# A transformer block on one core: other ends for the two sweeps of its down-projection

## Chip, cores and metric

One core of one Trainium2 chip runs the whole kernel. The metric is device time in microseconds (us); the kernel before takes 747.35 us, the median of three runs (747.33 to 748.2).

## The reference

The layer normalises x, projects it, runs two attention branches, and adds the gated result to x. Then comes the feed-forward part, with a causal convolution of width 3 over its hidden columns:

```python
def conv_glu(x, w_up, conv_w, conv_b, w_down):
    hid = x @ w_up
    hid = lax.conv_general_dilated(...) + conv_b
    gate, up = hid[..., :D_FF], hid[..., D_FF:]
    return (jax.nn.silu(gate) * up) @ w_down
...
x = x + mixed @ w_out
x = x + conv_glu(rms_norm(x, norm2_g), w_ffn_up, ffn_conv_w, ffn_conv_b, w_ffn_down)
```

x is 512 x 1024, D_FF is 2816, all float32. The case is about the last product, 512 x 2816 by 2816 x 1024, and the sum with x behind it.

## The kernel before, in words

**The product.** The 2816 rows of w_down are eleven pairs (i = 0 to 10) of 128 rows, the 1024 output columns two sweeps (s = 0, 1) of 512. One step, chunk `dn{s}_{i}`, adds the product of a 2 x 2 block matrix on either side by Strassen's scheme in Winograd's form: seven products P1 to P7 of sums of blocks instead of eight. The seven sums of the activations (`a{i}`, high and low parts) are made once, while the up-projection still runs, and serve both sweeps. Those of the weights are made per chunk.

**Precision.** Each float32 operand is split into a high part (a cast to fp32r) and a low part (the rest). A product is three matmuls: high by high (L855), high by low (L856), low by high (L857), each 128 x 128 by 128 x 256. With two halves t of the rows a product is six matmuls, a chunk 42, the stage 924. A product keeps its PSUM bank for a whole sweep, so seven of the eight banks are in use; sweep 1 takes the eighth and then those that sweep 0 has left.

**A weight chunk on its way.** SP issues its load (L100, 512 KB into `raw_dn`, two buffers). DVE forms the sums of blocks (L111 of 512 columns, L112 and L113 of 256). ACT casts the high part in two pieces, 768 and 1024 columns (L131), and DVE subtracts for the low part (L133). The 768 piece has P1, P3 and P2 and needs only the load; the 1024 piece has P5, P7, P6 and P4 and needs the sums. High and low have two buffers each (`whi`, `wlo`), so chunk c+2 can't be cast before PE is done with c. The load of chunk c+2 is issued behind the last low part of c, which frees its `raw` buffer.

**The ends of a sweep.** x (after the attention) lies in HBM as `x2d`. Four loads of 256 KB (L870) bring 512 of its columns into `xo`. When the last chunk of a sweep is done, `fin` adds the banks up into `xo`: ACT copies P1 to `u` (L891), DVE makes eleven or so adds (L884), and SP stores the result by quarters (L878, L915). `xo` has one buffer, so sweep 1's x waits for sweep 0's stores.

**The order.** The code gives only a rough order. A scheduler with a simulated timeline sets the order of each engine's instructions when the program is built; on the chip each engine keeps it strictly, and SP's loads and stores are one queue in that order. PE runs ahead with high-by-high matmuls of the next chunk where they are ready sooner than the low part. `behind(ins, others)` makes the scheduler put `ins` after `others`.

Of the kernel before, what the change touches and what calls it, by code (L numbers as in the profile page):

```python
# [8 lines left out]
F32 = mybir.dt.float32  # L9
F32R = mybir.dt.float32r  # L10
AF = mybir.ActivationFunctionType
ALU = mybir.AluOpType
# [3 lines left out]
P = 128  # L16
S = 512
D = 1024
NT = S // P
# [3 lines left out]
NP = NF // 2  # L23
# [41 lines left out]
def block_kernel(ctx: ExitStack, tc: tile.TileContext, x, xt, params, g2, rbx, wts, wdn, out):  # L65
# [25 lines left out]

    order = [key for key, _, _ in CHUNKS]

    raws, splits = {}, {}
    FIRST_DN = order.index("dn0_0")

    def load(i, parts=1):
# [10 lines left out]
    def down_sums(raw):  # L108

        b = raw.rearrange("p (b c) -> p b c", c=256)  # L110
        V.tensor_tensor(b[:, 4:6], b[:, 0:4:2], b[:, 0:2][:, ::-1], op=ALU.subtract)  # L111
        V.tensor_tensor(b[:, 6], b[:, 2], b[:, 4], op=ALU.subtract)  # L112
        V.tensor_tensor(b[:, 7], b[:, 6], b[:, 3], op=ALU.subtract)  # L113

    def split_gen(i, pieces):

        if i >= len(order):
            return
        key = order[i]
        kn = CHUNKS[i][1]  # L120
        raw = raws.pop(i)
        hi = wp.tile([P, 2048], F32R, tag="whi", name=f"whi_{key}")
        lo = wp.tile([P, 2048], F32R, tag="wlo", name=f"wlo_{key}")
        splits[key] = (hi.rearrange("p (k c) -> p k c", k=kn), lo.rearrange("p (k c) -> p k c", k=kn))
        cuts = [2048 // pieces * j for j in range(pieces + 1)]
        if i >= FIRST_DN:
            down_sums(raw)
            pieces, cuts = 2, [256, 1024, 2048]
        for j in range(pieces):
            sl = slice(cuts[j], cuts[j + 1])  # L130
            A.copy(hi[:, sl], raw[:, sl])  # L131
            E = G if i == 2 else V
            E.tensor_tensor(lo[:, sl], raw[:, sl], hi[:, sl].bitcast(F32), op=ALU.subtract)  # L133
            if j == pieces - 1 and i + 2 < len(order):
                next(load(i + 2))
            yield

    pos = {k: i for i, k in enumerate(order)}

    def run_chunk(key, body, pieces=4):  # L140

        sp = split_gen(pos[key] + 1, pieces)
        hi, lo = splits.pop(key)
        for _ in body(hi, lo):
            next(sp, None)
            yield
        for _ in sp:
            pass
# [29 lines left out]
    def ptile(tag, bufs, name):  # L178
        return pp.tile([P, S], F32, tag=tag, name=name, bufs=bufs)
# [553 lines left out]
    for _ in sp:  # L733
        pass
    ap_ctx.close()
    fp = ctx.enter_context(tc.tile_pool(name="fp", bufs=1))

# [88 lines left out]

    PRODS = (1, 6, 5, 7, 2, 4, 3)
    BLK = {1: 1, 3: 2, 2: 3, 5: 4, 7: 5, 6: 6, 4: 7}
# [4 lines left out]
    def pbank(name):  # L837
        tag = SLOTS[nslot[0] % 8]
        nslot[0] += 1
        return ptile(tag, BUFS[tag], name)  # L840

    def down_body(s, i, P_, fin):
        def body(hi, lo):
            a = pairs[i]
            for p in PRODS:
                if i == 0:
                    P_[p] = pbank(f"P{p}_{s}")
                ps = P_[p]
                for t in range(2):
                    o = 256 * OP[p] + P * t  # L850
                    sh, sl = a[:, o:o + P], a[:, 1792 + o:1792 + o + P]
                    mh, ml = hi[:, BLK[p], :], lo[:, BLK[p], :]
                    dst = ps[:, 256 * t:256 * (t + 1)]
                    first, last = i == 0, i == NP - 1
                    PE.matmul(dst, sh, mh, start=first and t == 0, stop=False, skip_group_check=True)  # L855
                    PE.matmul(dst, sh, ml, start=False, stop=False, skip_group_check=True)  # L856
                    PE.matmul(dst, sl, mh, start=False, stop=last, skip_group_check=True)  # L857
                if i == NP - 1:
                    fin(p)
                yield  # L860
        return body

    def sweep(s):
        P_ = {}
        col = 512 * s
        xt2 = fp.tile([P, NT, S], F32, tag="ub", name=f"xo{s}")

        def fetch():
            for t in range(NT):
                SP.dma_start(xt2[:, t, :], x2d[t, :, col:col + 512])  # L870

        def X(r, c):
            return xt2[:, 2 * r:2 * r + 2, 256 * c:256 * (c + 1)]

        def put(r, c):
            for t in range(2 * r, 2 * r + 2):
                cs = slice(256 * c, 256 * (c + 1))
                SP.dma_start(out[0, t * P:(t + 1) * P, col + 256 * c:col + 256 * (c + 1)], xt2[:, t, cs])  # L878

        tmp = {}  # L880
        v3 = lambda ap: ap.rearrange("p (t c) -> p t c", t=2)

        def add(o, a, b, op=ALU.add):
            V.tensor_tensor(o, a, b, op=op)  # L884

        def fin(p):
            ps = P_[p]
            p3 = v3(ps)
            if p == 1:
                tmp["u"] = fp.tile([P, S], F32, tag="cg", name=f"u2_{s}", bufs=1)  # L890
                A.copy(tmp["u"], ps)  # L891
                add(X(0, 0), p3, X(0, 0))
            elif p == 6:
                add(tmp["u"], ps, tmp["u"])
            elif p == 5:
                tmp["v"] = fp.tile([P, 768], F32, tag="st", name=f"u5_{s}", bufs=1)[:, 0:S]
                add(tmp["v"], ps, tmp["u"])
                add(X(0, 1), v3(tmp["v"]), X(0, 1))
                add(X(1, 1), v3(tmp["v"]), X(1, 1))
            elif p == 7:  # L900
                add(tmp["u"], ps, tmp["u"])
                add(X(1, 0), v3(tmp["u"]), X(1, 0))
                add(X(1, 1), p3, X(1, 1))
                put(1, 1)
            elif p == 2:
                add(X(0, 0), p3, X(0, 0))
                put(0, 0)
            elif p == 4:
                add(X(1, 0), X(1, 0), p3, op=ALU.subtract)
                put(1, 0)  # L910
            else:
                for t in range(2):
                    o = xt2[:, t, 256:512]
                    add(o, ps[:, 256 * t:256 * (t + 1)], o)
                    SP.dma_start(out[0, t * P:(t + 1) * P, col + 256:col + 512], o)  # L915

        for i in range(NP):
            if i == 6:
                fetch()
            for _ in run_chunk(f"dn{s}_{i}", down_body(s, i, P_, fin)):  # L920
                pass

    for s in range(2):
        sweep(s)


def _layout(inputs):
# [38 lines left out]
```

## Time and profile before

| what | value |
|---|---|
| median of three runs | 747.35 us |
| the profiled execution: its own time | 750.49 us |
| its span, first to last instruction | 747.8 us |
| PE busy in the span | 733.1 us (98%) |
| DVE busy | 536.0 us (72%) |
| ACT busy | 376.8 us (50%) |
| down-projection: first to last matmul start | 626.26 to 740.50 us |
| last add of DVE starts | 743.79 us |

Times on the timeline are us from the start of the span. A row of the timeline has the start, the length, the engine, the line and operation with what it writes and reads, and how many instructions stand in the row; in brackets is the idle time before it and what ended that. A line of the groups has the count, then the busy time and the mean ns of one, then the idle time before and what ended it. PE is matmul, PEld its weight load; SPq rows are the issue of a DMA, not the transfer. Busy times of matmuls overlap, so the step from one start to the next says more than their length.

### The profile page before, as it was taken

To read this page: it belongs to the slowest core of one execution; us is meant where nothing else is said; L and a number is where in the kernel's file an instruction comes from. 1 tells how busy PE (TensorE), PEld (TensorE's weight loads), DVE (VectorE), ACT (ScalarE), POOL (GpSimd) and SP (SyncE) were. 2 spreads that over 40 slices of the span, in tenths; PEclk is the share of its full clock that TensorE was granted. 3 is DMA by queue.
4 is the path that set the end of the run, shared out by engine and by line. 5 is a ranking of instruction groups with operands and counts; after the bars stand their busy time and mean duration, and the time that the engine had idled before them with its cause. 6 is when DMAs were issued, how large, how long until landed. Compare 5 with 4: busy or idle time off the path is not lost.

```text
span 747.8 us, 10959 instructions
## 1 busy us (share of the span) xinstructions
PE 733.1 (98%) x4301; PEld 645.1 (86%) x4301; DVE 536.0 (72%) x985; ACT 376.8 (50%) x671; POOL 41.8 (6%) x73
## 2 busy tenths in 40 slices
PE   9999999999999999999999999999999999998996
PEld 8999998888988888888899888888888889998896
DVE  6588876776978886573475777676668767878676
ACT  6675565557856775432254544534444433542341
POOL 2701200001011011000000000000000000000000
PEclk9999999999999999999999999999999999999999
DMA  8632232122221121235241232232133111443431
GB/s 295 250 122 85 79 116 74 61 88 79 65 106 57 57 99 71 85 113 224 114 169 61 110 112 75 96 112 103 67 113 113 61 53 57 141 142 122 159 109 62
DMA packets 19779, 79.96 MB, mean 107 GB/s; under 512 B 2192, under 2 KB 5392, under 8 KB 13584
## 3 DMA queue, kind: packets, MB, share of 16 engines
q1 hardware_dynamic: 19584, 79.18, 30.0%
q8 instruction: 33, 0.54, 0.3%
q14 instruction: 18, 0.15, 0.1%
q10 hardware_dynamic: 144, 0.10, 0.0%
HBM read 75.07 MB, written 4.19 MB: 106 GB/s over the span
## 4 chain that ended last, share of the span: by engine, by line
PE 89%; DMA 5%; DVE 4%; ACT 0%; SPq 0%; issue 0%; POOL 0%; ACTq 0%; DVEq 0%
PE pg L153 5%; PE pu L153 5%; PE pu L152 5%; PE pg L152 5%; PE pu L154 5%; PE pg L154 5%; PE P L856 3%; DMA raw_dn<-in_wdn 3%; PE P L857 3%; PE P L855 3%; PE gA L152 2%; PE wo L154 2%; PE wo L152 2%; PE wo L153 2%; PE gA L154 2%; PE qkB L152 2%
## 5 line engine op out<-in xcount | busy, mean ns | idle before, releaser
L133 DVE TENSOR_TENSOR wlo_up<-raw_up,whi_up 128x1024 fp32r<-128x1024 f32 (+1 forms) x50 | 52.4, 1093 | 49.6 <-ACT whi_up L131 49.6
L856 PE MATMUL P<-wlo_dn,a 128*128 128x256 f32 x308 | 83.2, 282 | 3.0 <-DVE wlo_dn L133 3.0
L857 PE MATMUL P<-whi_dn,a 128*128 128x256 f32 x308 | 82.8, 281 | 0.0
L855 PE MATMUL P<-whi_dn,a 128*128 128x256 f32 x308 | 76.6, 281 | 1.2 <-ACT whi_dn L131 1.2
L131 ACT CAST whi_dn<-raw_dn 128x768 fp32r<-128x768 f32 (+1 forms) x44 | 40.3, 943 | 63.2 <-PE P L857 38.2
L153 PE MATMUL pu<-htl,whi_up 128*128 128x512 f32 (+1 forms) x192 | 72.1, 375 | 0.0
L153 PE MATMUL pg<-htl,whi_up 128*128 128x512 f32 (+1 forms) x192 | 72.0, 375 | 0.0
L152 PE MATMUL pu<-hth,whi_up 128*128 128x512 f32 (+1 forms) x192 | 71.7, 374 | 0.0
L152 PE MATMUL pg<-hth,whi_up 128*128 128x512 f32 (+1 forms) x192 | 71.7, 374 | 0.0
L154 PE MATMUL pg<-hth,wlo_up 128*128 128x512 f32 (+1 forms) x192 | 71.1, 370 | 0.0
L154 PE MATMUL pu<-hth,wlo_up 128*128 128x512 f32 (+1 forms) x192 | 71.0, 370 | 0.0
L856 PEld LDWEIGHTS P<-wlo_dn,a 128*128 128x128 f32 x308 | 58.4, 191 | 3.5 <-DVE wlo_dn L133 3.4
L131 ACT CAST whi_up<-raw_up 128x1024 fp32r<-128x1024 f32 (+1 forms) x50 | 44.6, 945 | 29.9 <-PE pu L153 26.1
L857 PEld LDWEIGHTS P<-whi_dn,a 128*128 128x128 f32 x308 | 58.4, 191 | 0.0
L133 DVE TENSOR_TENSOR wlo_dn<-raw_dn,whi_dn 128x768 fp32r<-128x768 f32 (+1 forms) x44 | 47.6, 1088 | 12.3 <-ACT whi_dn L131 12.1
L855 PEld LDWEIGHTS P<-whi_dn,a 128*128 128x128 f32 x308 | 54.0, 190 | 2.2 <-ACT whi_dn L131 2.2
L152 PEld LDWEIGHTS pu<-hth,whi_up 128*128 128x128 f32 x192 | 36.0, 188 | 7.1
L152 PEld LDWEIGHTS pg<-hth,whi_up 128*128 128x128 f32 x192 | 36.0, 188 | 7.0
L154 PEld LDWEIGHTS pg<-hth,wlo_up 128*128 128x128 f32 x192 | 36.0, 188 | 6.7
L154 PEld LDWEIGHTS pu<-hth,wlo_up 128*128 128x128 f32 x192 | 36.0, 188 | 6.7
L153 PEld LDWEIGHTS pu<-htl,whi_up 128*128 128x128 f32 x192 | 36.1, 188 | 6.0
L153 PEld LDWEIGHTS pg<-htl,whi_up 128*128 128x128 f32 x192 | 36.1, 188 | 5.9
(239 smaller groups left out, 1922.0 us busy)
## 6 DMA issues: line engine op xcount, KB each, us to landing
raw_up<-in_wts SPq DMA_DIRECT2D x22, 1024.0 KB, 4.7
raw_dn<-in_wdn SPq DMA_DIRECT2D x22, 512.0 KB, 3.3
raw_gA<-in_wts SPq DMA_DIRECT2D x4, 1024.0 KB, 4.7
raw_qkB<-in_wts SPq DMA_DIRECT2D x4, 1024.0 KB, 4.7
raw_gB<-in_wts SPq DMA_DIRECT2D x4, 1024.0 KB, 4.7
raw_wo<-in_wts SPq DMA_DIRECT2D x4, 1024.0 KB, 4.7
xs<-in_xt SPq DMA_DIRECT2D x8, 256.0 KB, 4.6
xtok<-in_x SPq DMA_DIRECT2D x4, 512.0 KB, 8.4
```

What stands on the lines that cost most here:

```text
L131: A.copy(hi[:, sl], raw[:, sl])
L133: E.tensor_tensor(lo[:, sl], raw[:, sl], hi[:, sl].bitcast(F32), op=ALU.subtract)
L152: PE.matmul(ps, sh, mh, start=first, stop=False)
L153: PE.matmul(ps, sh, ml, start=False, stop=False)
L154: PE.matmul(ps, sl, mh, start=False, stop=last)
L855: PE.matmul(dst, sh, mh, start=first and t == 0, stop=False, skip_group_check=True)
L856: PE.matmul(dst, sh, ml, start=False, stop=False, skip_group_check=True)
L857: PE.matmul(dst, sl, mh, start=False, stop=last, skip_group_check=True)
```

## The change

1. The first sum of a chunk's weights is ordered behind the previous chunk's low parts (`behind`, L113).
2. Chunks dn1_5 to dn1_10 have their high and low parts in one tile `hl`, in the buffers that `a0` to `a7` leave, one for each chunk. Block 0 of `raw` is skipped in the split; the pieces stay 768 and 1024 columns.
3. P2 comes second in sweep 0, third in sweep 1.
4. Sweep 0's ends: ACT empties P1 (L888), P3 (L901), P7 (L897) and the negated P4 (L899); DVE adds P2, P6 and P5 from their banks (L868). What remains, four adds among `c`, `u` and `v`, four adds of x (four loads L879, now into the buffer of `a0`) and four stores of 256 KB (L918), is given out between the products from chunk dn1_1 on. x isn't fetched in the middle of either sweep any more.
5. The last two chunks of sweep 1 are written product by product, their ends (`fin1`) behind each; its x is fetched behind the last split, and one of the last stores is issued by ACT.

The core of the diff:

```diff
-        V.tensor_tensor(b[:, 4:6], b[:, 0:4:2], b[:, 0:2][:, ::-1], op=ALU.subtract)
+        ins = V.tensor_tensor(b[:, 4:6], b[:, 0:4:2], b[:, 0:2][:, ::-1], op=ALU.subtract)
+
+        behind(ins, late.get("halves", ()))
...
+            if i < FIRST_DN + NP + 5:
+                hi, lo = hi[:, 0:1792], lo[:, 0:1792]
+            else:
+                hl = late["pool"].tile([P, 3584], F32R, tag="ap", name=f"hl_{key}", bufs=8)
+                hi, lo = hl[:, 0:1792], hl[:, 1792:3584]
...
-    PRODS = (1, 6, 5, 7, 2, 4, 3)
+    PRODS = ((1, 2, 6, 5, 7, 4, 3), (1, 6, 2, 5, 7, 4, 3))
...
+    def fetch(name, col):
+        x = fp.tile([P, 3584], F32, tag="ap", name=name, bufs=8)[:, 0:2048].rearrange("p (t c) -> p t c", t=NT)
+        for t in range(NT):
+            SP.dma_start(x[:, t, :], x2d[t, :, col:col + 512])
+        return x
...
+    def fin0(p):
+        ps = banks[0][p]
+        c = tmp["c"]
+        if p == 1:
+            tmp["u"] = fp.tile([P, S], F32, tag="cg", name="u_0", bufs=1)
+            A.copy(tmp["u"], ps)
+        elif p == 2:
+            add(blk(c, 0, 0), v3(ps), v3(tmp["u"]))
+        elif p == 6:
+            add(tmp["u"], ps, tmp["u"])
+        elif p == 5:
...
+            add(tmp["v"], ps, tmp["u"])
+        elif p == 7:
+            A.copy(blk(c, 1, 1), v3(ps))
+        elif p == 4:
+            A.mul(blk(c, 1, 0), v3(ps), -1.0)
+        else:
+            A.copy(blk(c, 0, 1), v3(ps))
+
+    def rest0():
+        c, u, v = tmp["c"], tmp["u"], tmp["v"]
+        x = fetch("x_0", 0)
+        add(v3(u), v3(u), blk(c, 1, 1))
+        yield
+        add(blk(c, 1, 1), blk(c, 1, 1), v3(v))
+        yield
+        add(blk(c, 1, 0), blk(c, 1, 0), v3(u))
+        yield
+        add(blk(c, 0, 1), blk(c, 0, 1), v3(v))
+        yield
+        for t in range(NT):
+            add(c[:, t, :], c[:, t, :], x[:, t, :])
+            yield
+        for t in range(NT):
+            SP.dma_start(out[0, t * P:(t + 1) * P, 0:512], c[:, t, :])
...
+    for _ in split_gen(pos[f"dn1_{NP - 1}"], 2):
+        pass
+    tmp["x"] = fetch("x_1", 512)
+    ends = [(i, splits.pop(f"dn1_{i}")) for i in (NP - 2, NP - 1)]
+    for p in PRODS[1]:
+        for i, (hi, lo) in ends:
+            product(1, p, i, hi, lo)
+        fin1(p)
```

**What moves in the engines' order.** SP's queue around the start of sweep 1, before (`xo0`, `xo1` are the tiles of x of the two sweeps):

```order
L100 DMA raw_dn1_2_6434<-in_wdn 128x1024
L878 DMA out<-xo0_5867 128x256 x2
L100 DMA raw_dn1_3_6509<-in_wdn 128x1024
L915 DMA out<-xo0_5867 128x256 x2
L878 DMA out<-xo0_5867 128x256 x4
L870 DMA xo1_6485<-x2d_3786 128x512 x4
L100 DMA raw_dn1_4_6567<-in_wdn 128x1024
```

The same place in the changed program (`x_0` is the x of sweep 0, `c_0` its sums):

```order
L100 DMA raw_dn1_2_6429<-in_wdn 128x1024
L879 DMA x_0_6533<-x2d_3786 128x512 x4
L100 DMA raw_dn1_3_6490<-in_wdn 128x1024
L918 DMA out<-c_0_6192 128x512 x4
L100 DMA raw_dn1_4_6555<-in_wdn 128x1024
```

Four loads of x now stand between the loads of dn1_2 and dn1_3, and four larger stores ahead of dn1_4's. The buffer that `x_0` takes is that of `a0`, last read by the last matmul of P4 in dn1_0.

DVE at the seam, before (the numbers behind P are product and sweep; `u2`, `u5` are the sums from P1 and P6, and with P5):

```order
L133 TENSOR_TENSOR wlo_dn1_0_6419<-raw_dn1_0_6324,whi_dn1_0_6418 128x1024
L884 TENSOR_TENSOR xo0_5867<-P1_0_5868,xo0_5867 128x2x256
L884 TENSOR_TENSOR u2_0_6415<-P6_0_5882,u2_0_6415 128x512
L112 TENSOR_TENSOR raw_dn1_1_6377<-raw_dn1_1_6377 128x256
L884 TENSOR_TENSOR xo0_5867<-P2_0_5907,xo0_5867 128x2x256
L884 TENSOR_TENSOR u5_0_6442<-P5_0_5893,u2_0_6415 128x512
L113 TENSOR_TENSOR raw_dn1_1_6377<-raw_dn1_1_6377 128x256
L133 TENSOR_TENSOR wlo_dn1_1_6494<-raw_dn1_1_6377,whi_dn1_1_6493 128x768
L111 TENSOR_TENSOR raw_dn1_2_6434<-raw_dn1_2_6434 128x512
L884 TENSOR_TENSOR xo0_5867<-u5_0_6442,xo0_5867 128x2x256 x2
L884 TENSOR_TENSOR u2_0_6415<-P7_0_5900,u2_0_6415 128x512
L133 TENSOR_TENSOR wlo_dn1_1_6494<-raw_dn1_1_6377,whi_dn1_1_6493 128x1024
```

The same place in the changed program, from the low part 768 of dn1_1 to its low part 1024:

```order
L143 TENSOR_TENSOR wlo_dn1_1_6475<-raw_dn1_1_6373,whi_dn1_1_6474 128x768
L868 TENSOR_TENSOR u_0_6411<-u_0_6411,c_0_6192 128x512
L868 TENSOR_TENSOR c_0_6192<-c_0_6192,v_0_6444 128x2x256
L143 TENSOR_TENSOR wlo_dn1_0_6414<-raw_dn1_0_6320,whi_dn1_0_6413 128x1024
L111 TENSOR_TENSOR raw_dn1_1_6373<-raw_dn1_1_6373 128x512
L868 TENSOR_TENSOR c_0_6192<-c_0_6192,v_0_6444 128x2x256
L868 TENSOR_TENSOR c_0_6192<-c_0_6192,u_0_6411 128x2x256
L114 TENSOR_TENSOR raw_dn1_1_6373<-raw_dn1_1_6373 128x256
L115 TENSOR_TENSOR raw_dn1_1_6373<-raw_dn1_1_6373 128x256
L143 TENSOR_TENSOR wlo_dn1_1_6475<-raw_dn1_1_6373,whi_dn1_1_6474 128x1024
```

The low part 1024 of dn1_0 now stands behind the low part 768 of dn1_1, and the sums of dn1_1 come behind it; the adds that are left here read no bank, only `u`, `v` and `c`.

ACT at the same place in the changed program:

```order
L141 CAST whi_dn1_0_6413<-raw_dn1_0_6320 128x768
L888 COPY u_0_6411<-P1_0_5867 128x512
L901 COPY c_0_6192<-P3_0_5920 128x2x256
L897 COPY c_0_6192<-P7_0_5906 128x2x256
L899 ACTIVATE c_0_6192<-P4_0_5913 128x2x256
L141 CAST whi_dn1_1_6474<-raw_dn1_1_6373 128x768
L141 CAST whi_dn1_0_6413<-raw_dn1_0_6320 128x1024
L141 CAST whi_dn1_1_6474<-raw_dn1_1_6373 128x1024
L141 CAST whi_dn1_2_6539<-raw_dn1_2_6429 128x768
L141 CAST whi_dn1_3_6599<-raw_dn1_3_6490 128x768
```

Before, only the copy of P1 stood between the casts here, behind both pieces of dn1_0; now four bank copies stand ahead of the 768 piece of dn1_1. PE's order at the very end still goes chunk by chunk: all that is left of dn1_9 comes ahead of the last low-part products of dn1_10, which run P1, P2, P3, P6, P5, P7, P4.

More of the change, by code (lines that the diff above doesn't have):

```diff
@@ L92, in block_kernel @@
     order = [key for key, _, _ in CHUNKS]
-    raws, splits = {}, {}
+    raws, splits, late = {}, {}, {}
     FIRST_DN = order.index("dn0_0")
@@ L835, in block_kernel @@
     nslot = [0]
[L837 to L842, printed above, removed]
-        def body(hi, lo):
[L844 to L859, printed above, removed]
+    banks = [{}, {}]
@@ L860, in body, with down_body @@
+    rest = iter(())
+    def down_body(s, i):
+        def body(hi, lo):
+            for p in PRODS[s]:
+                product(s, p, i, hi, lo)
+                if s == 0 and i == NP - 1:
+                    fin0(p)
+                if s == 1 and i >= 1:
+                    next(rest, None)
                 yield
         return body
[L863 to L920, printed above, removed]
-                pass
```

82 lines of the change are left out of this document (73 added, 9 removed).

## The prediction

> **What bounds the kernel now.** I read the profile's page first, then the table by windows over the down-projection, which is all that the change touches. Columns: window, its length, busy time of PE, PEld, DVE, ACT and POOL with instructions, granted clock, DMA share, GB/s.
>
> ```profile
> 630.00:640.00 10.00, 9.67 (x81) 9.28 (x80) 9.87 (x17) 5.68 (x8) 0.00 (x0) 1.00 0.20 58
> 640.00:650.00 10.00, 9.73 (x86) 9.54 (x85) 7.06 (x10) 2.86 (x4) 0.00 (x0) 1.00 0.77 254
> 680.00:690.00 10.00, 7.77 (x57) 7.47 (x56) 10.00 (x20) 1.89 (x2) 0.00 (x0) 0.87 0.37 113
> 690.00:700.00 10.00, 9.42 (x76) 9.01 (x75) 6.34 (x9) 3.48 (x4) 0.00 (x0) 0.96 0.60 195
> 700.00:710.00 10.00, 9.23 (x81) 9.03 (x80) 6.18 (x10) 3.67 (x4) 0.00 (x0) 1.00 0.41 153
> 710.00:720.00 10.00, 10.00 (x87) 10.00 (x86) 6.92 (x11) 3.79 (x4) 0.00 (x0) 1.00 0.36 120
> ```
>
> PE is the bound, and it loses time in a few places only. At the seam of the two sweeps (680 to 690) DVE is full, ACT nearly idle and PE starved. The timelines give the places. First PE:
>
> ```profile
> 637.24 0.74 PE L855 MATMUL P<-whi_dn,a 128*128 128x256 f32 x4 [0.33 <-ACT whi_dn L131]
> 640.20 0.28 PE L856 MATMUL P<-wlo_dn,a 128*128 128x256 f32 x1
> 641.33 0.28 PE L856 MATMUL P<-wlo_dn,a 128*128 128x256 f32 x1
> 649.47 0.62 PE L855 MATMUL P<-whi_dn,a 128*128 128x256 f32 x3 [0.27 <-ACT whi_dn L131]
> 684.70 0.62 PE L855 MATMUL P<-whi_dn,a 128*128 128x256 f32 x4
> 687.55 0.58 PE L856 MATMUL P<-wlo_dn,a 128*128 128x256 f32 x1 [2.23 <-DVE wlo_dn L133]
> 690.71 0.33 PE L857 MATMUL P<-whi_dn,a 128*128 128x256 f32 x1
> 690.88 0.28 PE L856 MATMUL P<-wlo_dn,a 128*128 128x256 f32 x1
> 694.72 0.63 PE L855 MATMUL P<-whi_dn,a 128*128 128x256 f32 x3 [0.26 <-ACT whi_dn L131]
> 706.00 0.39 PE L856 MATMUL P<-wlo_dn,a 128*128 128x256 f32 x1 [0.77 <-DVE wlo_dn L133]
> 738.50 0.28 PE L855 MATMUL P<-whi_dn,a 128*128 128x256 f32 x1
> 739.68 0.28 PE L856 MATMUL P<-wlo_dn,a 128*128 128x256 f32 x1
> 740.50 0.28 PE L857 MATMUL P<-whi_dn,a 128*128 128x256 f32 x1
> ```
>
> Ten starts apart are 640.20 and 641.33 (a step of 113 ns) and 738.50 and 739.68 (118 ns). The width changes only at a PE gap; followed through the timeline, 401 of the 924 steps are wide, 1.8 us in all. The bracketed idle is from end to start; from start to start the excess over a step is larger. Between 685.04 (the fourth start of the group at 684.70) and 690.88 lie 16 steps: 5.84 us where 1.81 would do, so 4.0 lost, of which 2.4 is the gap and 1.6 the slow clock behind it. The same reckoning gives 0.9 at 637, 0.5 at 649, 0.2 at 684, 1.1 at 694 to 695 and 1.05 at 706. Seam (0.2, 4.0, 1.1): 5.3; all together 7.8 us.
>
> Why PE starved at 687: DVE had adds of sweep 0's ends ahead of the low half. Why at 649 and 706: a weight chunk queued behind four loads of the residual x.
>
> ```profile
> 680.54 0.68 DVE L884 TENSOR_TENSOR u<-P,u 128x512 f32<-128x512 f32 x1
> 681.14 0.41 DVE L112 TENSOR_TENSOR raw_dn<-raw_dn 128x256 f32<-128x256 f32 x1
> 681.47 0.68 DVE L884 TENSOR_TENSOR xo<-P,xo 128x512 f32<-128x512 f32 x1
> 686.28 1.22 DVE L133 TENSOR_TENSOR wlo_dn<-raw_dn,whi_dn 128x1024 fp32r<-128x1024 f32 x1
> 703.47 0.69 DVE L111 TENSOR_TENSOR raw_dn<-raw_dn 128x512 f32<-128x512 f32 x1 [4.60 <-DMA raw_dn<-in_wdn]
> ```
>
> ```profile
> 639.39 1.75 SPq L870 DMA_DIRECT2D xo<-x2d  x4
> 641.34 39.04 SPq L100 DMA_DIRECT2D raw_dn<-in_wdn  x9
> 695.20 1.75 SPq L870 DMA_DIRECT2D xo<-x2d  x4
> 697.00 14.19 SPq L100 DMA_DIRECT2D raw_dn<-in_wdn  x4
> ```
>
> ```profile
> 648.58 0.83 ACT L131 CAST whi_dn<-raw_dn 128x768 fp32r<-128x768 f32 x1 [2.50 <-DMA raw_dn<-in_wdn]
> ```
>
> ```profile
> raw_dn<-in_wdn SPq DMA_DIRECT2D x22, 512.0 KB, 3.3
> ```
>
> A chunk takes 3.3 us from issue to landing; issued 1.8 or 1.95 after the first x load it was used 703.47 - 695.20 = 8.3 and 648.58 - 639.39 = 9.2 us after that load, so it landed about 8.2 and 9.1 after it. The second time nothing but these five loads was in the queue; the first time another chunk was ahead.
>
> **The change, part by part.** Prices of single instructions (mean ns behind the bar):
>
> ```profile
> L133 DVE TENSOR_TENSOR wlo_dn<-raw_dn,whi_dn 128x1024 fp32r<-128x1024 f32 x21 | 25.6, 1221 | 1.9 <-ACT whi_dn L131 1.9
> L131 ACT CAST whi_dn<-raw_dn 128x1024 fp32r<-128x1024 f32 x21 | 22.0, 1050 | 11.6 <-DVE raw_dn L113 11.6
> L133 DVE TENSOR_TENSOR wlo_dn<-raw_dn,whi_dn 128x768 fp32r<-128x768 f32 x21 | 20.0, 954 | 8.8 <-ACT whi_dn L131 8.7
> L131 ACT CAST whi_dn<-raw_dn 128x768 fp32r<-128x768 f32 x21 | 17.6, 836 | 51.3 <-PE P L857 38.2 <-DMA raw_dn<-in_wdn 11.5 <-PE pu L153 1.6
> L748 ACT ACTIVATE ub<-pu,par 128x512 f32<-128x512 f32 x1 | 0.8, 766 | 0.0
> L891 ACT COPY u<-P 128x512 f32<-128x512 f32 x2 | 1.2, 580 | 2.9 <-PE P L857 2.9
> ```
>
> Back to back, the next one starts 0.1 us before this length is over (adds of 0.68 start 0.60 apart, those of 0.42 0.33).
>
> *The seam.* Four bank copies go to ACT, and only three adds stay ahead of dn1_1's high halves. Five stalls remain, each the producer's queue minus the matmuls that PE has in hand (13 or so per 1.5 us). (1) P1 of dn1_1: the 768 cast stands behind the negated P4 on ACT; from the last sweep-0 matmul 0.4 to be seen, 0.7 for the ACTIVATE, 0.85 for the cast, against 12 steps (1.4): 0.55. (2) P6 of dn1_0: the 1024 cast follows it, 0.95 against two steps: 0.7. (3) P6 of dn1_1: its 1024 cast waits for the last sum of dn1_1, behind DVE's low half 768, u+c, c+v, low half 1024, first sum, two more adds and two sums: 0.87 + 0.6 + 0.6 + 1.13 + 0.6 + 1.2 + 0.75 = 5.75, then 1.05 of cast; it begins 1.0 before stall (2) ends and PE has 46 steps (5.2): 6.8 - 1.0 - 5.2 = 0.6, with handovers 0.75. (4) dn1_2's 768 cast comes next, 0.8 against four steps: 0.3. (5) the low half after (3), 1.25 against seven steps and (4): 0.2. Together 2.5 where 5.3 was: **-2.8**. No gap is over 0.8, so I charge no slow clock. If the nearest rows mislead (a copy out of PSUM at 0.77 like the ACTIVATE, or a handover longer by 0.1 in each), it is 3.5; 1.9 below.
>
> *The load of x for sweep 0.* It leaves the stretch around 640: the stall at 649 shrinks from 0.5 to 0.2 (**-0.3**; between -0.5 and 0). It is now four loads into the buffer of a0, so SP waits at them until the last matmul of dn1_0 has read a0, and the load of chunk dn1_3 is queued behind them. Call E the moment at which that matmul's end is seen. The x loads start at E and dn1_3's load 1.8 later (dn1_1's low half 1024, which frees its buffer, ends about then too: one step, stall (3) and 1.2 after the matmul). It lands at E + 8.2 by the row at 695.20, E + 9.1 by the one at 639.39; with 0.85 of cast its high half is there at E + 9.05. PE has 42 more steps before it needs that half (4.8) and stalls (3), (4) and (5), 1.25, less the 0.35 that E lies behind the matmul's start: E + 5.7. **A new gap of 3.4 us** (2.6 if the five loads move 10% faster; 4.3 by 9.1). The low half 768 (0.95) comes after three matmuls: 0.45 more. The gap is longer than the 2.4 that was followed by 1.6 of slow clock, so I add 1.4 for that (1.1 to 1.7; 0 if it stays granted). **+5.25** (3.0 to 6.5).
>
> The Trainium skill ("TensorE: Matmul & The Clock Gate", Part 1, the table of the two states) has the half clock follow at least one idle window of about 3.4 us. The trace disagrees, since 2.4 us was enough; by the page a gap of 3.4 could stay at full clock, and the sum would be 1.4 lower.
>
> *dn1_4.* Its load is issued behind dn1_2's low half 1024, which now comes after dn1_3's 768: E + 9.05 + 0.95 + 1.2 with a handover, so E + 11.3; alone it lands at E + 14.6 and its high half is there at E + 15.5. PE has 46 steps after the new gap (5.2) and the two items just named (1.85): E + 16.1, no stall. But the four stores of c (1 MB) are issued in that gap, each once its x load has landed. Priced like the x loads (8.2 - 3.3 over four: 1.2 each, behind the five loads) they end at about E + 13, the chunk lands 1 later than alone, and PE waits 0.4. I take that where 1.05 was: **-0.65** (-1.05 to +0.5).
>
> *Order behind the low halves, and P2 in second place.* The stall at 637 grows, since P2's last matmul frees dn0_0's high buffer later: 0.9 to 1.1, **+0.2** (-0.1 to +0.4). In the steady chunks the low halves gain slack; PE is already full there (710 to 720), so nothing. From dn1_5 the halves have buffers of their own and run ahead, covered by the same PE time; without this cover it would be the cost of a normal chunk, nothing.
>
> *The end.* In the code it is product by product, but PE's order still finishes chunk dn1_9 before dn1_10, so DVE does not get its banks earlier. The adds keep their number:
>
> ```profile
> 741.21 0.68 DVE L884 TENSOR_TENSOR u<-P,u 128x512 f32<-128x512 f32 x1
> 743.79 0.69 DVE L884 TENSOR_TENSOR xo<-xo,P 128x512 f32<-128x512 f32 x1
> ```
>
> The last add starts 3.3 behind the last matmul (740.50). In the new order u<-P6 can start 15 steps before that matmul, plus 0.4 (-1.4), and ahead of the last add stand seven adds of 512 and two of 256: 7 x 0.6 + 0.66 + 0.1 = 5.0. So 3.6: **+0.3** (0.1 to 1.0). The two stores behind it are the same.
>
> Sum: -2.8 - 0.3 + 5.25 - 0.65 + 0.2 + 0.3 = **+2.0**. The profiled execution takes 750.49 (span 747.8), 3.1 above the median of 747.35; I carry the difference over: 752.5 for the profiled execution, **749.35** for the median.
>
> **Rivals.**
> *dn1_3 is not held up.* If its load came 3.3 after its own issue, at E + 5.1, the half would be there at E + 5.95, the gap 0.25 and no slow clock: +0.7 in place of +5.25, in all -2.55, **744.8**. It decides from a landing before about E + 6.2, where gap and slow clock together come to what the sum allows (3.25). For it: five loads spread over 16 engines can overlap. Against it: twice in this trace the chunk behind x landed 6.4 to 7.1 after its issue. 0.12.
> *The clock stays granted* behind the new gap: -1.4, **747.95**. For: one gap is all that the trace has to go by, and the gaps of 0.5 to 1.05 left the clock at 1.00. Against: that one was shorter and did trigger it. 0.10. The page of the Trainium skill named above speaks for this rival, the row against it.
> *Step width.* The gaps move, and with them the stretches at 113 and 118 ns. All narrow gives -1.8, **747.55**, 0.08; all wide (523 more steps by 4.5 ns) +2.35, **751.7**, 0.12. Before had both in turn, so I expect a mix.
> *A second slow stretch,* at dn1_4 or the seam (stores of c holding dn1_4's load 1.6 longer, to a gap of 2, and the slow clock behind it): +1.6 and +1.6, **752.55**, 0.08. Against: the stores are issued while the gap lasts and are mostly through.
>
> **Numbers.** My forecast has 0.50. About 0.2% (1.5 us) is what a measurement of this kernel can tell. Faster: the first rival and an edge of the forecast, 0.13. Within: clock, narrow steps and the forecast below 748.85, 0.27. Slower: the rest, 0.60. The forecast's own terms, whose ends won't come together, give 747.2 to 751.5; reaching toward the first rival and the wide steps until 0.2 is left out: 746.3 to 752.5.
>
> **What would show it.** A PE gap of about 3.4 us ahead of dn1_3's first matmuls, put down to ACT's cast with a DMA behind it; x loads that start when P4 of dn1_0 ends; a granted clock below 0.9 in that 10 us window; five stalls under 1 us at the seam, and DVE no longer full there; the last add 3.6 behind the last matmul. I am wrong if dn1_3's half is ready when PE comes, if the seam still has a stall over 1.5, or if a stretch after dn1_5 stalls.

## Result and the profile after

The changed kernel takes 754.71 us (median of 4, 754.3 to 755.72) where the kernel before took 747.78 on the same chip (median of 4, 747.33 to 748.91): a ratio of 1.0092, 95% interval 1.0075 to 1.011. It is slower, as forecast, but by 6.9 us where 2.0 was forecast, and outside the range that was given (746.3 to 752.5). The profiled execution took 754.30 us (span 752.6), against 752.5 forecast for it.

The windows of the changed kernel, columns as in the prediction:

```profile
680.00:690.00 10.00, 8.88 (x72) 8.28 (x72) 7.36 (x13) 4.14 (x6) 0.00 (x0) 1.00 0.15 52
690.00:700.00 10.00, 6.15 (x46) 5.46 (x46) 7.03 (x11) 2.27 (x3) 0.00 (x0) 1.00 0.75 264
700.00:710.00 10.00, 9.50 (x68) 9.30 (x68) 5.95 (x10) 2.97 (x4) 0.00 (x0) 0.83 0.30 106
710.00:720.00 10.00, 10.00 (x87) 9.96 (x86) 7.34 (x11) 3.91 (x5) 0.00 (x0) 1.00 0.32 107
```

The seam (680 to 690) is better than before: PE 8.88 where 7.77, DVE no longer full. The stretch behind it is far worse: 6.15 where 9.42, and then a granted clock of 0.83. PE's timeline there and at the end:

```profile
683.75 0.51 PE L863 MATMUL P<-whi_dn,a 128*128 128x256 f32 x2 [0.44 <-ACT whi_dn L141]
689.81 1.36 PE L863 MATMUL P<-whi_dn,a 128*128 128x256 f32 x7 [0.56 <-ACT whi_dn L141]
698.79 0.61 PE L863 MATMUL P<-whi_dn,a 128*128 128x256 f32 x3 [3.47 <-ACT whi_dn L141]
699.78 0.38 PE L864 MATMUL P<-wlo_dn,a 128*128 128x256 f32 x1 [0.38 <-DVE wlo_dn L143]
707.14 0.62 PE L863 MATMUL P<-whi_dn,a 128*128 128x256 f32 x3 [0.50 <-ACT whi_dn L141]
713.40 0.28 PE L865 MATMUL P<-whi_dn,a 128*128 128x256 f32 x1
714.53 0.28 PE L865 MATMUL P<-whi_dn,a 128*128 128x256 f32 x1
720.00 0.28 PE L863 MATMUL P<-hl_dn,a 128*128 128x256 f32 x1
721.20 0.28 PE L863 MATMUL P<-hl_dn,a 128*128 128x256 f32 x1
744.48 0.28 PE L865 MATMUL P<-hl_dn,a 128*128 128x256 f32 x1
```

The seam's two largest stalls are the rows at 683.75 and 689.81, the gap ahead of dn1_3 is that at 698.79, and dn1_4's that at 707.14. The last five rows hold something the forecast had not: ten steps take 1.13 us while the operands come from `whi` and `wlo` (713.40 to 714.53), and 1.20 once they come from `hl` (720.00 to 721.20), with no gap of note between. SP, ACT and DVE around the new gap and at the end:

```profile
689.33 1.75 SPq L879 DMA_DIRECT2D x<-x2d  x4
691.17 0.38 SPq L100 DMA_DIRECT2D raw_dn<-in_wdn  x1
```

```profile
680.84 0.59 ACT L897 COPY c<-P 128x512 f32<-128x512 f32 x1 [1.77 <-PE P L865]
681.43 0.60 ACT L899 ACTIVATE c<-P 128x512 f32<-128x512 f32 x1
688.71 1.78 ACT L141 CAST whi_dn<-raw_dn 128x1024 fp32r<-128x1024 f32 x2 [5.02 <-DVE raw_dn L115]
697.90 1.78 ACT L141 CAST whi_dn<-raw_dn 128x768 fp32r<-128x768 f32 x2 [7.41 <-DMA raw_dn<-in_wdn]
```

```profile
748.07 0.68 DVE L868 TENSOR_TENSOR x<-x,P 128x512 f32<-128x512 f32 x1
```

The chunk behind the four loads of x is cast at 697.90, 8.57 us after the first of them; in the two rows that the forecast went by it was 8.3 and 9.2. The bank copies take 0.59 and 0.60 (the rows for their price were 0.58, and 0.77 for the negated one). The casts at 688.71 had waited 5.02 for a sum on DVE, which leads to the stall at 689.81. The last add starts 3.59 us behind the last matmul.

Against the profiled execution of before (750.49), the 3.81 us more are: PE gaps +2.74, wide steps +1.80, the tail behind the last matmul +0.82, a first down-projection matmul that comes 0.55 earlier, and 1.0 less outside the span. (Gaps: the excess over 113.3 ns of all steps of 130 ns or more; wide steps: that of the steps between 115.5 and 130.)

### The profile page after: what moved, and what is told of

Read it like the earlier page. It is cut to its first block, busy times and chain, and to the rows that moved or that the text cites. A ratio compares the mean times of both kernels' runs of the same rounds, so it can differ in the third digit from the quotient of the medians.

```text
span 752.6 us, 10963 instructions
## 1 busy us (share of the span) xinstructions
PE 736.9 (98%) x4301; PEld 649.0 (86%) x4301; DVE 536.0 (71%) x984; ACT 378.4 (50%) x674; POOL 42.1 (6%) x73
## 4 chain that ended last, share of the span: by engine, by line
PE 95%; DMA 2%; DVE 1%; ACT 1%; SPq 0%; issue 0%; DVEq 0%; ACTq 0%
PE pg L165 5%; PE pu L165 5%; PE pu L164 5%; PE pg L164 5%; PE pu L166 5%; PE pg L166 5%; PE P L863 4%; PE P L864 4%; PE P L865 4%; PE gA L164 2%; PE wo L166 2%; PE wo L164 2%; PE wo L165 2%; PE gA L166 2%; PE qkB L164 2%; PE qkB L166 2%
## 5 line engine op out<-in xcount | busy, mean ns | idle before, releaser
L864 PE MATMUL P<-wlo_dn,a 128*128 128x256 f32 x224 | 59.8, 284 | 0.4 <-DVE wlo_dn L143 0.4
L865 PE MATMUL P<-whi_dn,a 128*128 128x256 f32 x224 | 59.5, 283 | 0.0
L863 PE MATMUL P<-whi_dn,a 128*128 128x256 f32 x224 | 51.5, 288 | 5.6 <-ACT whi_dn L141 5.5
L141 ACT CAST whi_dn<-raw_dn 128x768 fp32r<-128x768 f32 (+1 forms) x32 | 29.2, 941 | 47.4 <-DVE raw_dn L115 25.9
L143 DVE TENSOR_TENSOR wlo_dn<-raw_dn,whi_dn 128x768 fp32r<-128x768 f32 (+1 forms) x32 | 34.8, 1090 | 23.4 <-ACT whi_dn L141 23.2
L863 PEld LDWEIGHTS P<-whi_dn,a 128*128 128x128 f32 x224 | 37.3, 192 | 7.3 <-ACT whi_dn L141 7.2
L864 PEld LDWEIGHTS P<-wlo_dn,a 128*128 128x128 f32 x224 | 43.0, 192 | 0.7 <-DVE wlo_dn L143 0.6
L865 PEld LDWEIGHTS P<-whi_dn,a 128*128 128x128 f32 x224 | 43.1, 192 | 0.0
```

Source lines behind the costliest of these rows:

```text
L143: ins = E.tensor_tensor(lo[:, sl], raw[:, sl], hi[:, sl].bitcast(F32), op=ALU.subtract)
```

## Experiments

After the traces the account was this. The load of x ahead of dn1_3's chunk costs about 6 us, the tiles `hl` about 1.5 by wider steps, and the profile of before was taken from an execution longer than its median. The rival account was that any busy seam loses about as much somewhere, so that stalls come back elsewhere when one is taken away, and that the steps widen by chance. A and B in the expectations are the two answers to the question of each run. The runs were made on several chips; each ratio is to the kernel before on the same chip, where its median was 748.66 (e1 to e4), 748.89 (e5 to e8) and 748.82 (e9 to e12).

### e1: the kernel before, once more

> The kernel before once more, unchanged, for a second profile. Its first profiled execution took 750.49 us, 2.7 above the median of its runs (747.78). Theory A (step width): the extra lies in the wide matmul steps (401 of 924 in the first profile, 1.8 us) and this execution, if it takes about 747.5, has nearly all steps at 113 ns and a span near 745. Theory B: widths are the same again and what differed lies outside the down-projection; then the down stage takes 114.2 us from first to last matmul start again.

No edit. This execution took 747.09 us (span 745.4), 3.40 less than the first. Its seam:

```profile
686.40 0.38 PE L856 MATMUL P<-wlo_dn,a 128*128 128x256 f32 x1 [2.23 <-DVE wlo_dn L133]
686.62 0.29 PE L857 MATMUL P<-whi_dn,a 128*128 128x256 f32 x1
686.75 0.28 PE L855 MATMUL P<-whi_dn,a 128*128 128x256 f32 x1
```

The same stall of 2.23 us is there, but the steps behind it are 0.22 and 0.13: the slow clock that followed it in the first profile (1.6 us) is absent. Other small waits, such as two of 0.24 and 0.05 us late in the sweep, make up for part of that.

The down-projection is 1.42 shorter (0.84 of it fewer wide steps, 221 where the same count gives 411 for the first profile; 0.59 gaps), what lies ahead of it 1.0, what lies outside the span 1.0. Neither answer holds whole: the widths are a quarter of the difference, and more than half of it lies outside the down-projection. So most of what the first profile had above the median was particular to that execution, and is no constant to be carried over. This second execution is no typical one either: it lies 1.6 below the median of 21 runs on its chip (746.97 to 750.21).

### e2: the load of x_0 behind the last chunk

```diff
-        x = fetch("x_0", 0)
...
+    def rest1():
+        c, x = tmp["c"], fetch("x_0", 0, (late["load"],))
...
+            behind(add(c[:, t, :], c[:, t, :], x[:, t, :]), late["halves"])
```

> The changed kernel, but the four loads of x for sweep 0, the adds of x and the stores are moved behind the load of the last chunk and its low halves. Theory A (the queue place of the x loads is the main loss): the gaps ahead of dn1_3 (3.6 over a step, then 0.55 at the low half and 1.6 of slow clock) and of dn1_4 (0.67) go, 6.4 us; the end pays up to 1 for the adds of x: 749.3, within 748.3 and 750.3. Theory B (the loss is the wider steps and the end, and the queue only shows where PE would wait anyway): stalls come back at later chunks and the time stays above 752.

748.8 us (median of 11), ratio 1.0 (0.9991 to 1.0009). The gap ahead of dn1_3 shrinks to

```profile
695.46 0.62 PE L863 MATMUL P<-whi_dn,a 128*128 128x256 f32 x3 [0.54 <-ACT whi_dn L141]
```

and the clock is 1.00 in every window of the stage. The place of that load costs 754.71 - 748.8 = 5.9 us (6.9 by the ratios; the adds of x and the stores of sweep 0 moved with the load). Of the 6.0 between the spans of the two profiles 5.4 are gaps with the slow clock, the stalls at dn1_3 and dn1_4 above all; 1.4 are fewer wide steps, most of them in the first sweep, which the edit does not touch; and the tail gives 0.9 back (the last add is 3.99 behind the last matmul).

### e3: without the hl tiles

On top of e2:

```diff
-        if i < FIRST_DN + NP + 5:
+        if i < FIRST_DN + 2 * NP:
```

> As the run before it in this list, but chunks dn1_5 to dn1_10 keep their halves in the two whi and wlo buffers instead of the hl tiles; DVE, ACT, SP and PE have the same order as there. Theory A (operands in the hl tiles make the matmul step 120 ns instead of 118 or 113): 0.5 to 1.6 us faster than with hl tiles, and no step of 120 ns. Theory B (120 ns comes from something else, such as the phase after the last small gap): no difference over 0.3, steps near 120 remain.

747.4 us (median of 11), ratio 0.9989 (0.9978 to 1.0): 1.4 less than e2 by the medians, on the same chip; by the ratios it is 0.8, and their intervals touch. In the profiles the wide steps cost 1.3 less, in part because that stretch happened to fall into the 113 width; at 118 it would be about 0.5 (an estimate: 252 steps by 2.1 ns). The stretch that ran at 120 ns runs at 113 now:

```profile
720.00 0.28 PE L863 MATMUL P<-whi_dn,a 128*128 128x256 f32 x1
721.13 0.28 PE L863 MATMUL P<-whi_dn,a 128*128 128x256 f32 x1
```

### e4: x_0's loads just behind dn1_3's instead of ahead

```diff
-        x = fetch("x_0", 0)
+        x = fetch("x_0", 0, (late["load"],))
```

> The changed kernel with the x loads of sweep 0 put one place later, behind the load of dn1_3. Theory A (a queue place with slack is what is needed, not this swap): the gap ahead of dn1_3 goes, but the load of dn1_4 and the low half of dn1_2, which now stand behind x, are late: about 1.9 at dn1_2's low products, 2.2 and 0.7 at dn1_4, 1.4 at dn1_5; in all no faster than 753. Theory B (only dn1_3's load was hurt): 749.

752.83 us (median of 4), ratio 1.0064 (1.0048 to 1.0079). The gap ahead of dn1_3 falls to 0.87 us (the first row), and the low half of dn1_2 and the casts of dn1_5 pay (the other two):

```profile
696.25 0.62 PE L863 MATMUL P<-whi_dn,a 128*128 128x256 f32 x3 [0.87 <-ACT whi_dn L141]
697.84 0.58 PE L864 MATMUL P<-wlo_dn,a 128*128 128x256 f32 x1 [0.96 <-DVE wlo_dn L143]
710.64 0.61 PE L863 MATMUL P<-hl_dn,a 128*128 128x256 f32 x3 [0.80 <-ACT hl_dn L141]
```

The first two of these gaps, both under 1 us, brought the slow clock again. Windows of 3.41 us, up to the point where the granted clock falls and behind it:

```profile
694.25:697.67 3.42, 1.75 (x13) 1.34 (x11) 1.72 (x2) 0.83 (x1) 0.00 (x0) 1.00 0.69 251
697.67:701.08 3.41, 3.24 (x15) 3.25 (x16) 3.41 (x7) 0.00 (x0) 0.00 (x0) 0.50 0.80 284
```

Only 1.9 of the 5.9 come back, and 1.6 of what is left is this slow clock. Moved by one place, the loads hold up other chunks; behind the last one they hold up none. So the price belongs to the loads standing among the chunks, not to dn1_3.

### e5, e6: is it the tile or its address?

The tiles `hl` begin 64 bytes past a multiple of 128 bytes in the partition; `whi` and `wlo` begin on a multiple. e5 is e2 with the high part in `hl` and shifted by 16 words, the low part left in `wlo`; e6 is e3 with every `whi` and `wlo` shifted off by the same 64 bytes.

```diff
-                hi, lo = hl[:, 0:1792], hl[:, 1792:3584]
+                hi, lo = hl[:, 16:1808], lo[:, 0:1792]
```

> As e2_x0_late, but in chunks dn1_5 to dn1_10 only the high parts lie in the hl tiles, 64 bytes further on, and the low parts in the two wlo buffers. In the built program the hl tiles start 64 bytes past a multiple of 128 bytes of a partition; whi and wlo start at a multiple of 128. Theory A (alignment: a moving operand that starts 64 bytes off takes 120 ns a step): with the shift the high parts are aligned and no stretch is at 120 ns; 747.4, as e3_x0_late_whi. Theory B (place: operands beside the a tiles are slower): the steps with a high part as moving operand, two of three, stay at 120 and the stage at over 118 on average there; 748.3.

```diff
-                hi, lo = hi[:, 0:1792], lo[:, 0:1792]
+                hi, lo = hi[:, 16:1808], lo[:, 16:1808]
```

> As e3_x0_late_whi, but the high and low parts of all 22 chunks start 64 bytes further on in whi and wlo, so that they are off a multiple of 128 bytes, at the old place otherwise. Theory A (alignment): all stretches of the down-projection are at about 120 ns, 923 steps by 5.4 ns over e3's mean of 114.6: 5 us slower, 752.4. Theory B (place): no change, 747.4, steps at 113 and 118.

Ten starts apart each in e5, first out of `whi` and `wlo`, then out of `hl` and `wlo` (the high parts come from `hl` throughout from 709.89 on):

```profile
708.64 0.28 PE L864 MATMUL P<-wlo_dn,a 128*128 128x256 f32 x1
709.77 0.28 PE L864 MATMUL P<-wlo_dn,a 128*128 128x256 f32 x1
710.95 0.28 PE L864 MATMUL P<-wlo_dn,a 128*128 128x256 f32 x1
```

and in e6, out of `whi`, early in the first sweep:

```profile
650.04 0.28 PE L865 MATMUL P<-whi_dn,a 128*128 128x256 f32 x1
651.25 0.28 PE L865 MATMUL P<-whi_dn,a 128*128 128x256 f32 x1
```

With `hl` on the multiple no stretch is at 120 any more, but at 117; with `whi` off it every stretch is at 120. So the address alone is enough to bring 120 (e6). It is not all that the tile does: in e5 the step goes from 113 to 117 just where `hl` begins, without a gap and with only the high parts there, so that of the 6.6 ns between `hl` in e2 and `whi` some 2.5 go with the shift and some 4 stay. What these come from is not shown. In time: e5 748.59 (median of 10; ratio 1.0001, 0.9992 to 1.001) is no faster than e2, against the 747.4 of theory A; in its profiled execution 282 steps of the first sweep were 118 wide as well, but one execution does not explain a median. e6 is at 750.1 (median of 10; 1.0021, 1.0012 to 1.003), 2.7 slower than e3 by the medians and 2.4 by the ratios. Its wide steps cost 5.0 more, but the waits shrink by 1.0 and the tail by 1.0: a slower PE waits less. The two widths of 113 and 118 without any shift stay unexplained.

### e7: the tail, by another load order and GpSimd

On top of e3 the x of sweep 1 is loaded ahead of x_0, and the four adds of x_0 go to GpSimd:

```diff
-            add(c[:, t, :], c[:, t, :], x[:, t, :])
+            G.tensor_tensor(c[:, t, :], c[:, t, :], x[:, t, :], op=ALU.add)
```

> As e3_x0_late_whi, but x of sweep 1 is loaded ahead of x of sweep 0, and GpSimd makes the four adds of x into sweep 0's sums, of about 1.3 us each. In e3 the last add started 5.0 behind the last matmul, in the changed kernel 3.6. Theory A (the four adds on VectorE are what lengthened the end): 3.6 to 3.7 again, 1.3 faster: 746.1. Theory B (GpSimd's adds slow VectorE's, or their stores, now last in the queue, set the end): no gain, 747.4 or more.

748.14 us (median of 11), ratio 0.9995 (0.9985 to 1.0006): no gain. The last add is still 5.0 behind the last matmul (742.61 and 737.61), though DVE has four adds (2.49 us in all) less to do.

### e8: without the rule on the sums

On top of e3:

```diff
-        behind(ins, late.get("halves", ()))
```

> As e3_x0_late_whi, without the rule that puts a chunk's first sum behind the previous chunk's low parts; the scheduler orders VectorE freely. Theory A (the rule helps the seam): stalls of a microsecond and more come back at dn1_0 to dn1_2, 749 or more. Theory B (the copies on ScalarE are what helps the seam, and the rule only costs): the five seam stalls (2.4) fall to about 1.6, with 0.4 and 0.7 at dn1_8 and dn1_9: 747, within 0.7 of e3.

**741.76 us** (median of 5, 740.97 to 742.25), ratio 0.9913 (0.99 to 0.9927): faster than both kernels, and much more than expected. Windows of e8:

```profile
680.00:690.00 10.00, 10.00 (x90) 10.00 (x90) 8.17 (x14) 3.85 (x5) 0.00 (x0) 1.00 0.30 107
690.00:700.00 10.00, 9.08 (x80) 8.88 (x80) 8.61 (x12) 3.92 (x5) 0.00 (x0) 1.00 0.31 106
```

PE does not starve at the seam at all (one stall of 1.2 us follows at 692.82). Waits of the stage (engine and what it writes, releaser, total us, count, longest), e3 first:

```profile
ACT whi_dn L141 <- DVE raw_dn L115: 43.8, 17, 5.0
DVE wlo_dn L143 <- ACT whi_dn L141: 24.2, 22, 3.2
ACT whi_dn L141 <- PE P L865: 6.1, 8, 3.2
```

Then e8, whose lines are one lower:

```profile
ACT whi_dn L140 <- PE P L864: 39.3, 16, 3.3
DVE wlo_dn L142 <- ACT whi_dn L140: 11.6, 13, 2.9
ACT whi_dn L140 <- DVE raw_dn L114: 7.4, 6, 3.0
```

With the rule ACT's casts wait for DVE's sums 17 times (43.8 us), and DVE for the casts 22 times: each chunk's sums start only behind the previous low half, so the two engines take turns. Without it ACT waits mostly for PE to give a buffer back: it is ahead of PE. SP's queue of loads is in the same order in both. PE's order changes: at the end five of the last chunk's seven products are through ahead of P4 and P3, where e3 ends with low-part matmuls of P6, P5, P7 and P4 in turn. So DVE gets its banks one after the other, and the tail shrinks:

```profile
732.82 0.28 PE L864 MATMUL P<-whi_dn,a 128*128 128x256 f32 x1
```

```profile
735.22 0.67 DVE L867 TENSOR_TENSOR x<-x,P 128x512 f32<-128x512 f32 x1
```

2.4 us where e3 has 5.0. Of the 5.6 us between e3 and e8, 3.5 are the stage up to its last matmul (107.03 for 110.52) and 2.6 the tail; its first matmul comes 0.45 later.

### e9, e12: the rule by itself

e9 is the changed kernel without the rule and with nothing else; e12 is the kernel before with only the rule added.

> The changed kernel without the rule on the first sum; its x loads, hl tiles and end stay. Theory A (rule and x loads hurt the same chunks and do not add: with x still loaded at the start of sweep 1, stalls at dn1_2 and dn1_4 of 1.6 to 1.8 take the place of the one at dn1_3, and hl keeps its 120 ns): 753, within 1.5. Theory B (the two losses add, as e2 to e8 would suggest): 5 to 6 faster than the changed kernel, 749.

e9: 751.33 us (median of 10, 749.12 to 754.13), ratio 1.0035 (1.0021 to 1.0049). The rule costs 3.4 in the changed kernel (4.3 by the ratios) and 5.6 in e3. The time lies between the two answers; that the losses overlap is not clear of the noise of these runs. The comparison is not clean either: the order of SP's queue moves as well, to two loads of x ahead of dn1_3's and two behind, and one long gap becomes several shorter ones, among them

```profile
693.43 0.39 PE L863 MATMUL P<-wlo_dn,a 128*128 128x256 f32 x1 [0.97 <-DVE wlo_dn L142]
```

```diff
-        V.tensor_tensor(b[:, 4:6], b[:, 0:4:2], b[:, 0:2][:, ::-1], op=ALU.subtract)
+        ins = V.tensor_tensor(b[:, 4:6], b[:, 0:4:2], b[:, 0:2][:, ::-1], op=ALU.subtract)
+        behind(ins, late.get("halves", ()))
```

> The kernel before with nothing but the rule on the first sum added. Theory A (the rule costs by itself, chiefly as it moves the order of loads and sums): a stall of about 3 ahead of dn1_3, 1.9 and 0.9 at dn1_0 and dn1_1 in place of 2.4 at dn1_1: 2 to 4 slower than before, 752. Theory B (it only costs together with the other parts): within 1 of before.

e12: 752.42 us (median of 10, 749.51 to 754.4), ratio 1.0036 (1.0019 to 1.0052) to a before of 748.82: 2.7 slower by the ratio, 3.6 by the medians. Two stalls of over 2 us stand where before has one:

```profile
685.73 0.38 PE L859 MATMUL P<-wlo_dn,a 128*128 128x256 f32 x1 [2.00 <-DVE wlo_dn L134]
699.39 0.62 PE L858 MATMUL P<-whi_dn,a 128*128 128x256 f32 x3 [2.54 <-ACT whi_dn L132]
```

The rule costs by itself, with nothing else of the change there. The waits of the stage turn as they do between e8 and e3:

```profile
ACT whi_dn L132 <- DVE raw_dn L114: 45.8, 17, 7.1
ACT whi_dn L132 <- PE P L860: 8.1, 8, 3.2
```

Before, ACT waited 11.6 us for these sums and 38.2 for PE. Here too SP's queue moves with the rule (two stores ahead of dn1_2's load, six stores and two loads of x ahead of dn1_3's). The pair with the same queue is e3 and e8.

### e10: what ScalarE's copies are worth

On top of e8 three of the four bank copies go back to VectorE (P3, P7 and the negated P4):

```diff
-            A.copy(blk(c, 1, 1), v3(ps))
+            V.tensor_copy(blk(c, 1, 1), v3(ps))
...
-            A.mul(blk(c, 1, 0), v3(ps), -1.0)
+            V.tensor_scalar_mul(blk(c, 1, 0), v3(ps), -1.0)
```

> As e8_no_behind, but VectorE makes the three bank copies of P3, P7 and P4 at the seam that ScalarE makes there. Theory A (ScalarE's copies are what the change gains at the seam): stalls of 0.2 to 0.6 at dn1_0 to dn1_2 and 0.4 to 0.6 at each chunk behind, and the end in the order by chunk: 3 to 6 slower, 745 to 748. Theory B (VectorE has the time): no change, 741.8.

751.85 us (median of 10), ratio 1.0041 (1.0029 to 1.0054): 10 more than e8, and slower than before. It is too much for three copies. The stage is 5.1 longer (112.10), with

```profile
709.01 0.62 PE L862 MATMUL P<-whi_dn,a 128*128 128x256 f32 x3 [1.59 <-ACT whi_dn L140]
```

some 20 us behind the seam, and the tail is 5.5 again instead of 2.4, though nothing of the end was edited: PE's order there is chunk by chunk again, as in e3. SP's queue is that of e8. So the copies on ScalarE are needed for e8's time, in part through the order that they bring about; the 10 us are not their price alone.

### e11: e8 with the changes of e7

> As e8_no_behind, with x of sweep 1 loaded first and GpSimd's adds of x, as in e7_x1_first_pool. Theory A (VectorE's four adds of c, 2.4 us before the last ones, still hold up the end): the last add starts 0.8 nearer to the last matmul: 741.0. Theory B (the end is set by P3, last of the products, and the two stores): 741.8, no change.

742.31 us (median of 4), ratio 0.9909 (0.9891 to 0.9926): the same as e8, as in e7. The adds of x_0 on VectorE are hidden in either order.

## Why the prediction was right in sign and wrong in size

Taken apart along the chain of kernels that were run, the change is: before 748.8, e8 741.8 (ScalarE's bank copies, deferred adds, x out of the sweeps and all else of the change: -7.0), the rule on the sums +5.6 (e3), the `hl` tiles +1.4 (e2), x_0 ahead of dn1_3's load +5.9, which gives 754.7. The medians come from different chips; by the ratios, each to before on its own chip, the steps are -6.5, +5.7, +0.8 and +6.9, which give the +6.9 of the result. Each step is the price in that order of undoing: the rule's is 3.4 to 4.3 where x_0 and `hl` are still in place (e9), and the -7.0 hangs on the order of instructions that comes with it (e10).

- **The seam: right.** 2.5 us of stalls forecast where 5.3 were, 2.4 measured (0.40, 0.72, 0.84, 0.28, 0.17 against 0.55, 0.7, 0.75, 0.3, 0.2), without slow clock. But the 5.3 that this is taken from belong to one execution: 1.6 of them were slow clock, and in e1 the same stalls come to 3.8. So 1.5 of the 2.8 forecast here is no gain of the change. And the largest of the stalls that are left waits for a first sum that the rule holds back. I counted that wait at the seam and called the rule's own cost nothing; in e8, without it, all five are gone and one of 1.2 follows.
- **x_0 ahead of dn1_3: right in mechanism, 0.7 short.** 5.25 forecast (gap 3.4, low half 0.45, slow clock 1.4), 5.99 measured (3.63, 0.55 and 1.60, with 0.2 in double steps behind the waits). The chunk was used 8.57 behind the first load of x, within the bounds of 8.3 and 9.2. e2 shows the whole price of the place, 5.9 to 6.9. The rivals "dn1_3 is not held up" and "clock stays granted" fell.
- **dn1_4: 0.67, 0.4 forecast. The stall at 637: 1.09, 1.1 forecast. 649: 0.17, 0.2 forecast.** Right, or within the range given for the term.
- **The end: the add right, the tail not.** 3.6 forecast, 3.59 measured. But the span ends 4.5 behind the last add's start where before had 4.0; these 0.5 I can't account for. In e2 and e3, whose instructions stand in the same order, it is 5.0 and 4.0, so it varies with nothing moved.
- **The step that failed first is "I carry the difference over".** The profiled execution of before lay 3.1 above the median; its excess was in a slow clock, in wide steps and outside the stage (e1), things that the changed kernel does not inherit. The sum was 1.8 short for the profiled execution (754.30 to 752.5), the forecast 5.4 short for the median. The other 3.6 are this step: it set the median 3.1 below the profiled execution, and it came out 0.4 above. (The 747.35 was the median of three runs only; over 21 to 27 runs on each chip of the experiments before's median was 748.7 to 748.9.) What the sum missed were 1.8 us of wide steps, 1.0 of gaps and 0.5 of the tail, less 1.5 for an earlier start of the stage and less time outside the span. Against e1 the change is +7.21: gaps +3.33, wide steps +2.64, tail +0.77, and a first matmul 0.47 later.
- **"Before had both in turn, so I expect a mix" failed.** The `hl` tiles hold the width at 120 for the six last chunks, and 282 steps of the first sweep fell to 118, which no edit explains: +1.80 against the first profile, +2.64 against e1. I looked at the buffers of the tiles, not at what reading from them costs; 0.8 to 1.4 us of it is theirs (e3).
- **"PE is already full there, so nothing" failed in its reach.** PE is full between 710 and 720 in the changed kernel as before, and still the rule costs 3.4 (e9) to 5.6 (e8). The words put its price at nothing. This isn't what the sum missed: the rule's stalls at the seam and the end chunk by chunk stood in the orders and were priced there. What stayed hidden was that without the rule, with x_0's loads last and without the `hl` tiles, the change is faster than before (e8). In the trace of before ACT's 768 casts waited mostly for PE (38.2 us in the quoted row); in the changed kernel the waits of the stage read

```profile
ACT whi_dn L141 <- DVE raw_dn L115: 25.9, 10, 5.0
ACT whi_dn L141 <- PE P L865: 10.1, 7, 3.1
```

The lead of the producers is what the rule spends, and a full PE in one window does not show it. That ACT and DVE taking turns is what empties PE's reserve at the seam is read from these waits; that dropping the rule ends both (e8), and that adding it to the kernel before brings the turns (e12), is shown.

**The slow clock.** The forecast charged it to the new gap because 2.4 us had been enough before. How much idle it takes can be read from the traces. In each, the granted clock changes only at points that lie whole multiples of 3.41 us apart (687.40, 690.81 and 745.43 in before), and it is low for one such stretch at a time while PE works. The stretches that hold the long gaps, of before, e1, the changed kernel and e12, each with the clock of that stretch itself:

```profile
683.99:687.40 3.41, 1.33 (x10) 1.11 (x9) 3.41 (x5) 0.18 (x1) 0.00 (x0) 1.00 0.00 0
684.78:688.19 3.41, 1.79 (x15) 1.79 (x16) 3.41 (x7) 0.00 (x0) 0.00 (x0) 1.00 0.25 73
696.84:700.25 3.41, 1.08 (x7) 0.89 (x8) 2.24 (x4) 1.78 (x2) 0.00 (x0) 1.00 0.53 202
697.77:701.18 3.41, 1.79 (x15) 1.80 (x16) 2.41 (x4) 0.86 (x2) 0.00 (x0) 1.00 0.44 170
```

In these stretches PE was busy 1.33 us in before, 1.08 in the changed kernel and 1.75 in e4 (two gaps of 0.87 and 0.96), and the next stretch was granted 0.50. It was busy 1.79 in e1 and in e12, where an edge of the stretches cuts the gap in two, and the clock stayed at 1.00: the same gap of 2.23 us costs 1.6 us more or nothing, by where it falls. A gap of 3.47 leaves at least 1.73 us of one stretch idle, wherever the edges lie, so charging it was sound; that before's seam had it was chance. The border is not exact: a stretch at the end of e10 with 1.56 busy was followed by 1.00. The Trainium skill's page "TensorE: Matmul & The Clock Gate" (Part 1) has the half clock follow an idle window of some 3.4 us, and the window free-running. The traces agree with windows that run free of the kernel, and disagree on the idle: 1.66 us in one of them was enough (e4).

## What to carry to other kernels

A single profiled execution that lies well above the median is no base: what this one had above was not passed on to the changed kernel. A bulk load that isn't urgent goes behind the last urgent one on its queue, since everything queued behind it pays; moving it by one place here only moved the stall. An order rule between two engines that feed each other is judged by who waits for whom: if the producer's waits turn from "for the bound engine" to "for the other producer", it has lost its lead, even where the bound engine is still full.

## What the runs showed of the hardware

- A matmul of 128x256 whose moving operand begins 64 bytes past a multiple of 128 bytes took 120 ns a step (`hl` in e2, `whi` and `wlo` in e6), on the multiple 113 to 118 (e3, e5). Reading six chunks out of `hl` cost 0.8 to 1.4 us (e2 to e3), and of the 6.6 ns a step between the two places some 2.5 went with the address (e5). The Trainium skill's page "SBUF — State Buffer" (Operand start alignment) lets an operand start at any multiple of its element and says that this is about legality, not speed; the runs add the speed.
- The granted clock fell to 0.50 for 3.41 us after a stretch of 3.41 us in which PE was busy 1.75 us or less, and not after 1.79 (with the one exception in e10); two gaps of under 1 us in one stretch were enough (e4).
- As long as the operands stay in `whi` and `wlo`, the widths 113 and 118 change only at PE gaps, and one execution falls into the one or the other (221 and 411 wide steps of the same program). The times of before spread from 746.97 to 751.07, those of e6, where every step is 120, from 749.76 to 750.93. That the widths make part of the spread fits this, and is not shown.
- Making PE slower by 5.0 us (e6) cost 2.4 to 2.7: what waits on others gives part of it back.
